# A hybrid RWKV-7 and RG-LRU layer on one core: row halves in turn, a padded matrix, other operand offsets, chunks and first loads

## The chip, the cores and the metric

The kernel runs on one core of a Trainium2 chip. The metric is device time in microseconds of one execution, the median of several runs. Engines are named as the profile names them: PE is TensorE's matmul, PEld its load of the stationary operand, DVE is VectorE, ACT is ScalarE, POOL is GpSimd, SP is SyncE, which issues nearly all DMAs.

## What is computed

One decoder layer over 256 tokens of width 2048: half a SwiGLU step, a mixing step with two groups of heads that share one input and one output projection, another half SwiGLU step, and a norm.

```python
h = h + 0.5 * swiglu(rms_norm(h, ffn1_norm), w_gate, w_up, w_down)     # 2048 -> 5632 -> 2048
p = rms_norm(h, mix_norm) @ w_in                                       # 2048 -> 5408
r, xw, k, v, xa, xg = split(token_shift(p[..., :3360]), (1024, 64, 1024, 1024, 64, 160))
w = -softplus(-(w0 + tanh(xw) @ w2)) - 0.5       # decay, low rank 64
a = sigmoid(a0 + xa @ a2)                        # rate, low rank 64
g = sigmoid(xg) @ g2                             # gate, low rank 160
y_rwkv = delta_rule_scan(r, exp(-exp(w)), k, v, a) * g                 # 16 heads of 64
y_lru = gated_linear_recurrence(p[..., 3360:])
h = h + concat(y_rwkv, y_lru) @ w_out                                  # 2048 -> 2048
h = h + 0.5 * swiglu(rms_norm(h, ffn2_norm), w_gate2, w_up2, w_down2)
return rms_norm(h, final_norm)
```

## The kernel before

**Products in three parts.** Weights and activations are float32. For the large products each is split into a high part in the format fp32r and a low part that holds the rest, and a product is high x high + high x low + low x high: three matmuls that add up in one PSUM bank. `weights` (line 47) loads a strip of a weight matrix, k tile by k tile (128 rows), into a `wst` buffer; ScalarE copies it to `whi` (line 73), VectorE subtracts to get `wlo` (line 74). There are three buffers of each. `kstep` k tiles share one DMA, `kop` k tiles one split.

**The large products.** In `rows_times` (line 85) a 128x128 block of the activations is stationary and up to 512 columns of weights move: used by both FFNs and by w_out. Each matmul there loads another stationary block than the one before or loads it again. In `columns_times` (line 97) the weights are stationary and 256 tokens move: the projections by w_in.

**The FFN** (line 164). The 5632 hidden columns are taken in chunks: four of 1024, then two of 768, each cut into pieces of at most 512. A chunk's gate product runs over 16 k tiles and 2 token tiles, then its up product. The product's hidden tile is transposed on TensorE (line 183, four transposes per k pair) in the middle of the next chunk's gate product, after k tile 7; the last chunk's after k tile 11 of the down product. The down product runs over 44 k tiles in pieces of 1024 or 512 columns.

**The start.** x comes in four quarters of 512 columns, which are transposed in halves (line 126, 16 transposes each, with the split to `xahi` and `xalo` on ScalarE and VectorE behind them). The first chunk's weights follow with k tiles 0 and 1 alone, then in pairs.

**The mixing stage** (line 825) runs steps of two halves of the heads in the order of line 874, between the eleven projections. `decays` (line 457) makes decay and rate: w2 lies on rows 0 to 63 of `w2a2`, a2 on rows 64 to 127, and each float32 matmul over 64 rows and 256 tokens is issued as two passes. `small()` hands out PSUM banks 6 and 7 in turn, `small(True)` banks 3 to 5. The gram products (line 574) and the chain of the recurrence (line 683 and on) also work on 64 rows. `rwkv_out` (line 722) multiplies by the gate: two matmuls for each of 8 blocks, over 128 rows of `g2a` and 32 rows of `g2b`.

**What sets the order.** A scheduler orders each engine's instructions from the program order and priorities. `high_priority(offset)` lets what is inside go ahead by that many places; `issue_after(x)` keeps it behind x. Each engine then works through its queue in order.

**Where tiles lie.** In the built program's memory map the bytes per partition are these: on the left, from below, `const` with `junk` (2048 bytes) in it, then the weight buffers `wst` at 22400, `whi` at 46976, 51072 and 55168, `wlo` at 59264, 63360 and 67456, then `xahi` at 71552 and `xalo` at 87936. In the first FFN `hThi` lies at 128896 and `hTlo` from 173952 to 219008. On the right, downward from 229344: `h2` at 212960 (16384 bytes), then the second FFN's `xbhi` at 180192 and `xblo` at 196576. The second FFN's last left tile ends at 178048.

Of the kernel before, what the change touches and what calls it, by code (L numbers as in the profile page):

```python
# [3 lines left out]

# [7 lines left out]
F32 = mybir.dt.float32  # L12
# [8 lines left out]
class Core:  # L21


    def __init__(self, ctx, tc, S, D, WMAX):
# [11 lines left out]
        self.h = None  # L36
        self.ones = self.const.tile([P, P], F32, name="ones")
# [9 lines left out]
    def weights(self, pieces, ktiles, kstep=2, kop=1, head=False):  # L47
# [4 lines left out]
        steps = [1, 1] if head else []  # L52
        while sum(steps) < len(ktiles):
            steps.append(min(kstep, len(ktiles) - sum(steps)))
        for k0, n in zip(itertools.accumulate([0] + steps), steps):
            with self.tc.high_priority(offset=4000):
# [11 lines left out]
                for j in range(0, n, kop):  # L68
# [4 lines left out]
                    self.last_split = nc.scalar.copy(hi[:, : m * width], src)  # L73
                    nc.vector.tensor_tensor(  # L74
                        lo[:, : m * width], src, hi[:, : m * width].bitcast(F32), ALU.subtract
                    )
# [8 lines left out]
    def rows_times(self, banks, xhi, xlo, kidx, whi, wlo, width, first, last):  # L85

        nc = self.nc
        for t in range(self.NT):
# [5 lines left out]
            for n, c, w in cuts:  # L94
                nc.tensor.matmul(banks[t][n][:, :w], b, whi[:, c : c + w], start=False, stop=last)  # L95
# [30 lines left out]
    def transposed_half(self, hf, gT, xhi, xlo, banks):  # L126

        nc = self.nc
        per = self.NK // 2
        for j in range(0, per, 2):  # L130
            bk = self.bank(banks[(j // 2) % len(banks)])
            for jj in range(2):
                k = hf * per + j + jj
# [6 lines left out]
            for jj in range(2):  # L140
                k = hf * per + j + jj
                src = bk[:, jj * 256 : jj * 256 + self.S]
                nc.scalar.activation(xhi[:, k, :], src, AF.Copy, scale=gT[:, k : k + 1])
                nc.vector.scalar_tensor_tensor(  # L144
                    xlo[:, k, :], src, gT[:, k : k + 1], xhi[:, k, :].bitcast(F32), ALU.mult, ALU.subtract
                )

# [16 lines left out]
def ffn(core, xhi, xlo, rstd, wg, wu, wd, after_first, after_down, fpool, down, head=False):  # L164
# [4 lines left out]
    while c < DFF:  # L169
        left = DFF - c  # L170
        w = 1024 if left >= 2 * 1024 or left <= 1024 else left // 2
        w = min(w, left)
        chunks.append((c, w))
        c += w
# [22 lines left out]
    for c0, w in chunks:  # L197
# [3 lines left out]
        for i, (k, hi, lo) in enumerate(core.weights([(wg, c0, w)], ks, head=head and c0 == 0)):  # L201
            core.rows_times(gb, xhi, xlo, k, hi, lo, w, i == 0, i == NK - 1)
            if i == NK // 2 - 1:
                for f in pending:
                    f()
                pending = []
# [18 lines left out]
    for piece, (c0, w) in enumerate(down):  # L225
# [3 lines left out]
        for i, (k, hi, lo) in enumerate(core.weights([(wd, c0, w)], list(range(NF)), 2048 // w, 1024 // w)):  # L229
# [18 lines left out]
class Mix:  # L248
# [20 lines left out]
    def consts(self):  # L269
# [132 lines left out]
        self.g2b = mc.tile([32, 1024], F32, name="g2b")  # L402
        nc.sync.dma_start(out=self.g2a, in_=d["rwkv_g2"][0, 0:128, :])
        nc.sync.dma_start(out=self.g2b, in_=d["rwkv_g2"][0, 128:160, :])
# [638 lines left out]
```

## Time and profile before

| | |
|---|---|
| median of 3 runs | 1979.71 us (1976.21 to 1979.80) |
| the profiled execution | 1979.79 us, of which the span from the first to the last instruction is 1978.1 us |
| TensorE busy | 1952.5 us, 99% of the span |
| VectorE, ScalarE busy | 1078.4 us (55%), 880.1 us (44%) |
| granted TensorE clock, mean | 0.996 of full speed |

An engine that is busy all the time sets the time; what the others do counts where it waits for them. The records of a few matmuls are missing from the trace, so counts over a stretch are taken from the program and times from landmarks.

### The profile page before, as it was taken

Reading aid. Unit: us, or ns where it says so; the run is one execution under the profiler, and the core shown is the slowest. Engines: PE = TensorE matmul, PEld = TensorE weight load, DVE = VectorE, ACT = ScalarE, POOL = GpSimd, SP = SyncE. Lnnn points to the kernel's source line nnn. Section 1 sums busy time; section 2 is a strip of 40 time slices with the busy share of each in tenths; the row PEclk is TensorE's granted clock in tenths of the full one; section 3 lists DMA queues with packets and bytes.
Section 4 is the critical chain, followed back from the end, with each engine's and each line's share of the span. In section 5 each row is a group of like instructions: output and inputs, shape, how many; then the busy total and the mean of one; then the engine's idle time right before and its main releaser. Section 6 shows DMA issues by size and latency. Waiting matters only on the chain.

```text
span 1978.1 us, 26035 instructions
## 1 busy us (share of the span) xinstructions
PE 1952.5 (99%) x10789; PEld 1652.5 (84%) x10789; DVE 1078.4 (55%) x1313; ACT 880.1 (44%) x1062; POOL 8.9 (0%) x52
## 2 busy tenths in 40 slices
PE   8999999999999999999999999999999999999997
PEld 6888888888888889898899878888888888888886
DVE  4455444544545447886684875444545455544543
ACT  4544434444434335544354554434443444443443
POOL 0000000000000001000000000000000000000000
PEclk9999999999999999999999999999999999999999
DMA  6555555566656556544342365555555556665553
GB/s 234 192 189 194 182 196 181 167 189 180 209 187 211 191 187 219 164 139 126 97 147 88 127 224 183 189 192 174 188 187 175 181 175 178 207 214 193 193 192 128
DMA packets 128639, 354.51 MB, mean 179 GB/s; under 512 B 21023, under 2 KB 23272, under 8 KB 128392
## 3 DMA queue, kind: packets, MB, share of 16 engines
q1 hardware_dynamic: 128200, 351.79, 55.4%
q8 instruction: 84, 1.38, 0.3%
q10 hardware_dynamic: 320, 1.06, 0.1%
q14 instruction: 35, 0.29, 0.0%
HBM read 347.05 MB, written 5.77 MB: 178 GB/s over the span
## 4 chain that ended last, share of the span: by engine, by line
PE 97%; DVE 1%; ACT 1%; DMA 0%; issue 0%; SPq 0%; DVEq 0%; ACTq 0%
PE bank L92 26%; PE bank L95 26%; PE bank L93 26%; PE bank L104 4%; PE bank L106 4%; PE bank L105 4%; PE bank L183 1%; PE bank L574 1%; PE bank L502 1%; PE bank L467 0%; PE bank L663 0%; PE bank L135 0%; PE bank L691 0%; PE bank L670 0%; DMA wst<-in_ffn_w_gate_dram 0%
## 5 line engine op out<-in xcount | busy, mean ns | idle before, releaser
L74 DVE TENSOR_TENSOR wlo<-wst,whi 128x1024 fp32r<-128x1024 f32 (+1 forms) x680 | 795.5, 1170 | 834.1 <-ACT whi L73 832.9
L73 ACT CAST whi<-wst 128x1024 fp32r<-128x1024 f32 (+1 forms) x680 | 685.8, 1009 | 1004.5 <-PE bank L95 867.3
L92 PE MATMUL bank<-whi,xahi 128*128 128x512 f32 (+1 forms) x896 | 337.2, 377 | 3.8 <-DVE xalo L144 3.6
L93 PE MATMUL bank<-wlo,xahi 128*128 128x512 f32 (+1 forms) x896 | 330.1, 375 | 1.1 <-DVE wlo L74 1.1
L92 PE MATMUL bank<-whi,xbhi 128*128 128x512 f32 (+1 forms) x768 | 289.5, 377 | 0.0
L93 PE MATMUL bank<-wlo,xbhi 128*128 128x512 f32 (+1 forms) x768 | 283.7, 377 | 0.0
L92 PE MATMUL bank<-whi,hThi 128*128 128x512 f32 x704 | 274.2, 390 | 0.0
L93 PE MATMUL bank<-wlo,hThi 128*128 128x512 f32 x704 | 274.0, 389 | 0.0
L95 PE MATMUL bank<-whi,xalo 128*128 128x512 f32 (+1 forms) x896 | 264.8, 376 | 0.0
L95 PE MATMUL bank<-whi,hTlo 128*128 128x512 f32 x704 | 231.4, 389 | 0.0
L95 PE MATMUL bank<-whi,xblo 128*128 128x512 f32 (+1 forms) x768 | 227.6, 377 | 0.0
L92 PEld LDWEIGHTS bank<-whi,xahi 128*128 128x128 f32 x896 | 168.7, 188 | 41.2 <-DVE xalo L144 4.0
L104 PE MATMUL bank<-xahi,whi 128*128 128x256 f32 x688 | 198.6, 289 | 1.0 <-DVE raw L437 1.0
L106 PE MATMUL bank<-xahi,wlo 128*128 128x256 f32 x688 | 197.4, 288 | 0.0
L105 PE MATMUL bank<-xalo,whi 128*128 128x256 f32 x688 | 196.8, 286 | 0.0
L93 PEld LDWEIGHTS bank<-wlo,xahi 128*128 128x128 f32 x896 | 168.6, 188 | 31.9 <-DVE wlo L74 1.5
L95 PEld LDWEIGHTS bank<-whi,xalo 128*128 128x128 f32 x896 | 159.8, 189 | 24.9
L92 PEld LDWEIGHTS bank<-whi,xbhi 128*128 128x128 f32 x768 | 144.5, 188 | 34.3
L93 PEld LDWEIGHTS bank<-wlo,xbhi 128*128 128x128 f32 x768 | 144.4, 188 | 28.7
L95 PEld LDWEIGHTS bank<-whi,xblo 128*128 128x128 f32 x768 | 135.8, 189 | 23.4
L92 PEld LDWEIGHTS bank<-whi,hThi 128*128 128x128 f32 x704 | 132.2, 188 | 27.4
L93 PEld LDWEIGHTS bank<-wlo,hThi 128*128 128x128 f32 x704 | 132.2, 188 | 27.3
(242 smaller groups left out, 1355.3 us busy)
## 6 DMA issues: line engine op xcount, KB each, us to landing
wst<-in_ffn_w_down_dram SPq DMA_DIRECT2D x88, 1024.0 KB, 5.0
wst<-in_ffn_w_up_dram SPq DMA_DIRECT2D x64, 1024.0 KB, 5.0
wst<-in_ffn_w_gate_dram SPq DMA_DIRECT2D x63, 1024.0 KB, 5.0
wst<-in_w_in_dram SPq DMA_DIRECT2D x40, 1024.0 KB, 5.2
wst<-in_ffn_w_gate_dram SPq DMA_DIRECT2D x32, 768.0 KB, 4.4
wst<-in_ffn_w_up_dram SPq DMA_DIRECT2D x32, 768.0 KB, 4.4
wst<-in_w_out_dram SPq DMA_DIRECT2D x16, 1024.0 KB, 5.5
wst<-in_w_in_dram SPq DMA_DIRECT2D x4, 640.0 KB, 4.3
```

What stands on the lines that cost most here:

```text
L73: self.last_split = nc.scalar.copy(hi[:, : m * width], src)
L74: nc.vector.tensor_tensor(lo[:, : m * width], src, hi[:, : m * width].bitcast(F32), ALU.subtract)
L92: nc.tensor.matmul(banks[t][n][:, :w], a, whi[:, c : c + w], start=first, stop=False)
L93: nc.tensor.matmul(banks[t][n][:, :w], a, wlo[:, c : c + w], start=False, stop=False)
L95: nc.tensor.matmul(banks[t][n][:, :w], b, whi[:, c : c + w], start=False, stop=last)
L104: nc.tensor.matmul(out, a, xhi[:, k, :], start=first, stop=False, skip_group_check=True)
L105: nc.tensor.matmul(out, a, xlo[:, k, :], start=False, stop=False, skip_group_check=True)
L106: nc.tensor.matmul(out, b, xhi[:, k, :], start=False, stop=last, skip_group_check=True)
L183: nc.tensor.transpose(bk[:, jj * 256 + t * P : jj * 256 + (t + 1) * P], hid[:, t, (j + jj) * P : (j + jj + 1) * P], core.ident,)
L502: self.nc.tensor.matmul(bk[0:8, :256], ind[:, j0 + j, :], src[:, j * 256 : (j + 1) * 256], start=j == 0, stop=j == 3)
L574: nc.tensor.matmul(bks[par][:, j * P : (j + 1) * P], BK[j // 2][rows, j % 2, c, :], KR[j // 2][rows, j % 2, c, :], start=True, stop=True,)
```

## The change

- `decays` takes the four blocks in pairs and issues a decay product (rows 0 to 63, a bank of `small(True)`) and a rate product (rows 64 to 127, a bank of `small()`) in turn.
- `g2b` becomes a tile of 128 rows, zero from row 32 on, and its matmul takes all 128 rows of the third block of the low-rank inputs.
- `junk` grows by 128 bytes and `h2` by 2016 bytes per partition, with no other use of them.
- The FFN's chunks are one of 512 columns and then five of 1024.
- `kop` and `kstep` follow from the width: 1 and 2 k tiles for 1024 columns, 2 and 4 for 512 and for 384. For the down product and the projections they come out as before.
- At the start the first weights, x's quarters and the next weights are issued in turn; x is transposed in quarters, the first ahead, each later one behind k tile 0, 1 or 2 of the first chunk; the splits of the first chunk's weights up to k tile 7 are kept behind the splits of x that `marks` holds.

```diff
@@ class Core
+        self.marks = []
...
-    def weights(self, pieces, ktiles, kstep=2, kop=1, head=False):
+    def weights(self, pieces, ktiles, head=False):
...
-        steps = [1, 1] if head else []
+        kop = self.WMAX // width
+        kstep = 2 * kop
+        steps = [1, 1, 2] if head else []
...
-            with self.tc.high_priority(offset=4000):
+            with self.tc.high_priority(offset={0: 9500, 1: 8700, 2: 8500}.get(k0, 4000) if head else 4000):
...
-                    self.last_split = nc.scalar.copy(hi[:, : m * width], src)
-                    nc.vector.tensor_tensor(
-                        lo[:, : m * width], src, hi[:, : m * width].bitcast(F32), ALU.subtract
-                    )
+                    with ExitStack() as behind:
+                        if head and 0 < k0 < 8:
+                            for mark in self.marks[4 * k0 - 1 if k0 < 3 else -1]:
+                                behind.enter_context(self.tc.issue_after(mark.ins))
+                        self.last_split = nc.scalar.copy(hi[:, : m * width], src)
+                        nc.vector.tensor_tensor(
+                            lo[:, : m * width], src, hi[:, : m * width].bitcast(F32), ALU.subtract
+                        )
...
-    def transposed_half(self, hf, gT, xhi, xlo, banks):
+    def transposed(self, k0, n, gT, xhi, xlo, banks):
...
+                self.marks.append((a, b))
...
@@ ffn
-        left = DFF - c
-        w = 1024 if left >= 2 * 1024 or left <= 1024 else left // 2
-        w = min(w, left)
+        w = (DFF - c) % 1024 or 1024
...
             core.rows_times(gb, xhi, xlo, k, hi, lo, w, i == 0, i == NK - 1)
+            if head and c0 == 0 and i in head:
+                with core.tc.high_priority(offset=3000), core.tc.issue_after(core.last_mm.ins):
+                    head[i]()
...
-        for i, (k, hi, lo) in enumerate(core.weights([(wd, c0, w)], list(range(NF)), 2048 // w, 1024 // w)):
+        for i, (k, hi, lo) in enumerate(core.weights([(wd, c0, w)], list(range(NF)))):
@@ Mix.consts
-        self.g2b = mc.tile([32, 1024], F32, name="g2b")
+        self.g2b = mc.tile([P, 1024], F32, name="g2b")
+        g.memset(self.g2b, 0.0)
...
-        nc.sync.dma_start(out=self.g2b, in_=d["rwkv_g2"][0, 128:160, :])
+        nc.sync.dma_start(out=self.g2b[0:32], in_=d["rwkv_g2"][0, 128:160, :])
@@ Mix.decays
-        for half, dst, bias in ((0, ld, self.w0h), (1, ta, self.a0h)):
-            rows = slice(64 * half, 64 * half + 64)
-            for j in range(0, 4, 2):
-                bk = self.small()
-                for a in range(2):
-                    jj = hf * 4 + j + a
+        for j in range(0, 4, 2):
+            bks = (self.small(True), self.small())
+            for a in range(2):
+                jj = hf * 4 + j + a
+                for half in range(2):
+                    rows = slice(64 * half, 64 * half + 64)
                     nc.tensor.matmul(
-                        bk[:, a * 256 : a * 256 + 256], self.w2a2[rows, jj * P : (jj + 1) * P],
+                        bks[half][:, a * 256 : a * 256 + 256], self.w2a2[rows, jj * P : (jj + 1) * P],
                         L[rows, 0, :], start=True, stop=True,
                     )
+            for a in range(2):
+                jj = hf * 4 + j + a
+                for bk, dst, bias in zip(bks, (ld, ta), (self.w0h, self.a0h)):
                     nc.scalar.activation(
...
@@ Mix.rwkv_out
-            nc.tensor.matmul(gb[:, :256], self.g2b[:, jj * P : (jj + 1) * P], L[0:32, 2, :], start=False, stop=True)
+            nc.tensor.matmul(gb[:, :256], self.g2b[:, jj * P : (jj + 1) * P], L[:, 2, :], start=False, stop=True)
@@ tile_hybrid_layer_kernel
-    junk = const.tile([P, HD], mybir.dt.bfloat16, name="junk")
+    junk = const.tile([P, HD + 64], mybir.dt.bfloat16, name="junk")
...
-                with tc.high_priority(offset=8000 if q < 2 else 0):
+                with tc.high_priority(offset=(9000, 8600, 8400, 8300)[q]):
...
-            with tc.high_priority(offset=8500):
-                norm_half(0, 0, *xa)
-            norm_half(0, 1, *xa)
+
+            def norm_quarter(q):
+                core.transposed(4 * q, 4, gT[:, :NK], *xa, ((2, 3), (4, 5), (6, 7))[q % 3])
+
+            with tc.high_priority(offset=8800):
+                norm_quarter(0)
...
-                first_norm, park, fpool, [(0, HD), (HD, HD)], head=True)
+                first_norm, park, fpool, [(0, HD), (HD, HD)], head={q: partial(norm_quarter, q + 1) for q in range(3)})
...
-        core.h = h2.tile([P, core.NT, D], F32, name="h2")
+        core.h = h2.tile([P, core.NT * D + 504], F32, name="h2")[:, : core.NT * D].rearrange("p (t d) -> p t d", t=core.NT)
```

## Rows read from the trace of the kernel before

**Rows 1.** The page: busy time by engine; the chain that ended last.

```profile
PE 1952.5 (99%) x10789; PEld 1652.5 (84%) x10789; DVE 1078.4 (55%) x1313; ACT 880.1 (44%) x1062; POOL 8.9 (0%) x52
...
PE 97%; DVE 1%; ACT 1%; DMA 0%; issue 0%; SPq 0%; DVEq 0%; ACTq 0%
```

**Rows 2.** Busy time in the mixing stage: stretch, its length, busy us by engine.

```profile
752.00:1177.00 425.00, 419.40 (x3621) 377.52 (x3620) 316.28 (x565) 213.61 (x312) 7.93 (x44) 0.99 0.47 147
```

**Rows 3.** Timeline of PE, start and length in us: first transposes of hidden tiles.

```profile
126.43 0.38 PE L183 MATMUL bank<-ident,hid 128*128 128x128 f32 x2
...
215.24 0.38 PE L183 MATMUL bank<-ident,hid 128*128 128x128 f32 x2
...
387.97 0.49 PE L183 MATMUL bank<-ident,hid 128*128 128x128 f32 x3
...
457.11 0.38 PE L183 MATMUL bank<-ident,hid 128*128 128x128 f32 x2
...
1335.99 0.38 PE L183 MATMUL bank<-ident,hid 128*128 128x128 f32 x2
...
1427.70 0.38 PE L183 MATMUL bank<-ident,hid 128*128 128x128 f32 x2
...
1605.38 0.38 PE L183 MATMUL bank<-ident,hid 128*128 128x128 f32 x2
...
1674.13 0.38 PE L183 MATMUL bank<-ident,hid 128*128 128x128 f32 x2
```

**Rows 4.** The chain in the first FFN's down product, at both ends of 384 matmuls.

```profile
541.84 1.31 PE bank L183 x12
...
630.67 0.16 PE bank L135
```

**Rows 5.** The chain at the first group of decay passes.

```profile
790.19 1.06 PE bank L467 x4
791.25 0.32 PE bank L104
791.56 0.12 PE bank L105
```

**Rows 6.** The chain at one block of the gate products.

```profile
998.73 0.43 PE bank L745 x2
999.16 0.62 PE bank L746 x2
999.78 0.32 PE bank L106
```

**Rows 7.** The chain at two groups of gram passes.

```profile
842.68 1.16 PE bank L574 x8
...
950.27 0.65 PE bank L574 x8
```

**Rows 8.** Timeline of POOL and of SP's queue: a memset, the load of g2b.

```profile
755.31 0.63 POOL L408 MEMSET lru_wa<- 64x512 f32 x1
...
790.74 0.49 SPq L404 DMA_DIRECT2D g2b<-in_rwkv_g_dram  x1
```

**Rows 9.** Timeline of the start, with the idle time before and its releaser.

```profile
5.10 4.01 PE L135 MATMUL bank<-ident,h 128*128 128x128 f32 x16 [1.09 <-DMA h<-in_x_dram]
...
7.14 1.57 PEld L135 LDWEIGHTS bank<-ident,h 128*128 128x128 f32 x8 [0.47 <-DMA h<-in_x_dram]
...
8.42 1.04 ACT L73 CAST whi<-wst 128x1024 fp32r<-128x1024 f32 x1 [5.86 <-DMA wst<-in_ffn_w_gate_dram]
...
9.50 1.23 DVE L74 TENSOR_TENSOR wlo<-wst,whi 128x1024 fp32r<-128x1024 f32 x1 [5.28 <-ACT whi L73]
...
10.64 0.48 DVE L144 SCALAR_TENSOR_TENSOR xalo<-bank,gT,xahi 128x256 fp32r<-128x256 f32 x1
...
12.70 0.79 PE L92 MATMUL bank<-whi,xahi 128*128 128x512 f32 x1 [3.59 <-DVE xalo L144]
```

**Rows 10.** The chain at the start.

```profile
13.49 0.43 PE bank L93
```

More of the change, by code (lines that the diff above doesn't have):

```diff
@@ L3 @@
 from contextlib import ExitStack
+from functools import partial
 import concourse.bass as bass
@@ L94, in rows_times @@
             for n, c, w in cuts:
-                nc.tensor.matmul(banks[t][n][:, :w], b, whi[:, c : c + w], start=False, stop=last)
+                self.last_mm = nc.tensor.matmul(banks[t][n][:, :w], b, whi[:, c : c + w], start=False, stop=last)
     def columns_times(self, bks, ntile, i, last, xhi, xlo, k, hi, lo):
@@ L124, in spread_rstd @@
         nc.vector.tensor_copy(self.rb, bk[:, :256])
-    def transposed_half(self, hf, gT, xhi, xlo, banks):
+    def transposed(self, k0, n, gT, xhi, xlo, banks):
         nc = self.nc
-        per = self.NK // 2
-        for j in range(0, per, 2):
+        for j in range(0, n, 2):
             bk = self.bank(banks[(j // 2) % len(banks)])
             for jj in range(2):
-                k = hf * per + j + jj
+                k = k0 + j + jj
                 for t in range(self.NT):
@@ L140, in transposed_half @@
             for jj in range(2):
-                k = hf * per + j + jj
+                k = k0 + j + jj
                 src = bk[:, jj * 256 : jj * 256 + self.S]
-                nc.scalar.activation(xhi[:, k, :], src, AF.Copy, scale=gT[:, k : k + 1])
-                nc.vector.scalar_tensor_tensor(
+                a = nc.scalar.activation(xhi[:, k, :], src, AF.Copy, scale=gT[:, k : k + 1])
+                b = nc.vector.scalar_tensor_tensor(
                     xlo[:, k, :], src, gT[:, k : k + 1], xhi[:, k, :].bitcast(F32), ALU.mult, ALU.subtract
                 )
+                self.marks.append((a, b))
     def sumsq(self, c0, w, acc, junk):
@@ L161, in rstd_of, with ffn @@
         nc.vector.reciprocal(rstd, tmp)
-def ffn(core, xhi, xlo, rstd, wg, wu, wd, after_first, after_down, fpool, down, head=False):
+def ffn(core, xhi, xlo, rstd, wg, wu, wd, after_first, after_down, fpool, down, head=None):
     nc, NT, NK, D, S = core.nc, core.NT, core.NK, core.D, core.S
@@ L200, in ffn @@
         gb = [[core.bank(t * nb + n) for n in range(nb)] for t in range(NT)]
-        for i, (k, hi, lo) in enumerate(core.weights([(wg, c0, w)], ks, head=head and c0 == 0)):
+        for i, (k, hi, lo) in enumerate(core.weights([(wg, c0, w)], ks, head=bool(head) and c0 == 0)):
             core.rows_times(gb, xhi, xlo, k, hi, lo, w, i == 0, i == NK - 1)
+            if head and c0 == 0 and i in head:
+                with core.tc.high_priority(offset=3000), core.tc.issue_after(core.last_mm.ins):
+                    head[i]()
             if i == NK // 2 - 1:
@@ L425, in project @@
             self.nproj += 1
-        for i, (k, hi, lo) in enumerate(core.weights(pieces, list(range(NK)), 4, 2)):
+        for i, (k, hi, lo) in enumerate(core.weights(pieces, list(range(NK)))):
             core.columns_times(bks, ntile, i, i == NK - 1, xhi, xlo, k, hi, lo)
@@ L933, in norm_half @@
     def norm_half(i, hf, xhi, xlo):
-        core.transposed_half(hf, gT[:, i * NK : (i + 1) * NK], xhi, xlo, (0, 1, 2, 3) if hf == 0 else (4, 5, 6, 7))
+        core.transposed(hf * NK // 2, NK // 2, gT[:, i * NK : (i + 1) * NK], xhi, xlo, (0, 1, 2, 3) if hf == 0 else (4, 5, 6, 7))
     def norm_rows(i, bank):
```

## The prediction

> **What bounds the kernel now.** I read the page's shares first: TensorE is busy 99% of the span, VectorE and ScalarE are not near it, and the chain that ended last is TensorE for 97% of its length [rows 1]. So the question for each edit is how many nanoseconds of TensorE's queue it removes; a faster transfer or eviction is worth nothing unless TensorE waits for it. The mixing stage looks busier with other things, so I asked for it alone: TensorE is busy 419.4 of 425.0 us there [rows 2], which leaves 5.6 us of waiting in all. A busy TensorE still need not run at its pace, so the next view is the pace: how long one weight-switching matmul takes in each stage.
>
> The pace comes from landmarks. Each chunk's hidden tile is transposed in the middle of the next chunk's gate product, so two neighbouring landmarks of 1024-wide chunks are 384 matmuls of 512 columns apart (half a gate, an up, half a gate: 96 + 192 + 96), and 16 transposes. Twelve of these take 1.31 us [rows 4], so sixteen 1.75. In the first FFN: 215.24 - 126.43 - 1.75 = 87.06 us, or 226.7 ns a matmul. In the second: 1427.70 - 1335.99 - 1.75 = 89.96 us, 234.3 ns [rows 3]. The reader should see that the same instructions with the same shapes take 7.6 ns more. The 768-wide chunks, cut into 512 + 256 columns, are 192 such pairs apart: (457.11 - 387.97 - 1.75) / 192 = 351.0 ns a pair in the first FFN, (1674.13 - 1605.38 - 1.75) / 192 = 349.0 in the second [rows 3]. One and a half 512-wide matmuls at 226.7 would be 340.0.
>
> **Why the second FFN is slower.** What differs is where the stationary operand lies. By the byte offsets told with the kernel, xa lies at 71552, a multiple of 128, xb at 180192, which is 96 beyond one. It is not the region: hThi and hTlo of the first FFN reach across it (128896 to 219008), and the down product that reads them needs (630.67 - 541.84 - 1.31) / 384 = 227.9 ns for k tiles 12 to 43, with 12 transposes at 109 ns taken off [rows 4]; the surplus over 226.7 is the two slow pieces at either end. So I take the odd offset as the cause.
>
> **The operands' offsets.** The 504 floats more in h2 put xb at 178176, and the 128 bytes more in junk move the weights and xa to 47104 and 71680: all multiples of 2048, and at the same distance from each other modulo 2048 as the first FFN's are now. So xb should take xa's pace. In the four 1024-wide chunks that is 4 x (89.96 - 87.06) = 11.6 us. For the pace at a multiple of 2048 itself the trace has no row (all fast operands lie 1920 beyond one); I take 226.7, the row of the same relative place.
>
> A rule of the Trainium skill speaks against this term: "SBUF — State Buffer", Specifications (TRN2), gives 16-byte cachelines as what an access pays for, and every offset here is a multiple of 32. By it moving xb changes nothing. The 7.6 ns of the rows above speak for some dependence that this rule doesn't have; it is the first rival.
>
> **The chunks.** 512 + 5 x 1024 in place of 4 x 1024 + 2 x 768: no 256-wide pieces. Per 768 chunk 192 x (351.0 - 340.0) = 2.1 us in the first FFN, 192 x (349.0 - 340.0) = 1.7 in the second; two each: 4.2 + 3.4 = 7.6 us. ScalarE and VectorE split the same columns (a 512-wide chunk is split two k tiles at a time), so the reserve of three split tiles is worth the same TensorE time. The projections, w_out and the down product get the steps that they had.
>
> **The decay and rate products.** 32 passes (16 fp32 matmuls of two passes), now in eight groups of four, all rows of a group in one half of the array. A group costs 1.06 us and its successor 0.32 instead of 0.12, so 1.26 [rows 5]; four passes at 0.216, half of what two passes over 128 rows take [rows 6], are 0.86, the rest is going into the 64-row form and out again. The change makes groups of eight, upper and lower in turn, each half with a bank of its own: four groups. Do halves run side by side? The gram products show both: eight passes in 1.16 us where one half's follow each other, 0.65 where the halves take turns [rows 7]. At that ratio, 0.56, eight decay passes cost 0.56 x (1.06 + 0.86) = 1.08, what four do now, and 4 x 1.26 = 5.0 us go. Bounds: 1.6 if nothing runs side by side (four switches of about 0.4 saved), 5.9 if the groups merge in pairs. I take 5.0, as the order in the program is that of the 0.65 row. The chain banks 3 to 5 are idle then, and ScalarE issues as many evictions.
>
> **Gate's second matrix.** Now two passes of 128 rows (0.43), two of 32 rows (0.62), and 0.32 for the successor [rows 6], which takes 0.12 elsewhere [rows 5]; with 128 rows 2 x 0.43 and 0.12. That is (0.62 - 0.43) + 0.20 = 0.39 us, eight times: 3.1. Lower bound 1.5, if the four of the second half only shorten TensorE's waiting. The padding adds a POOL memset of 128x1024; a 64x512 one takes 0.63 us [rows 8], so an estimate of 1.3 us, at about 755 us. SP's transfer of g2b waits for it, with the weight loads queued behind; but that transfer is issued at 790.74 [rows 8], 34 us later. Cost nothing; if the cover were gone, 1.3 us.
>
> **The first loads.** Now: x lands, 16 transposes run at 5.10, the first weights land at 8.42, and the first product starts at 12.70 because ScalarE and VectorE split weights between the evictions [rows 9]. The landmark gives the total: 126.43 less 2.5 x 43.5 us of products is 17.6 us lost at the front. After: 256 KB of weights precede x's first quarter. The second quarter, 512 KB more, is waited for until 7.14 [rows 9], 2.0 us behind the first, so 256 KB are 1.0 at most, and x lands between 5.1 and 6.1; I take 5.8. Four transposes (half of the 1.57 there), an eviction on each engine (0.48 on VectorE, and about the same ahead of it on ScalarE, rows 9) and the first product starts near 7.9. Six matmuls at the early 0.43 [rows 10], then quarters' transposes between k tiles: k 1 at 12, k 2 at 15 to 16 (its split now queues behind quarter 1's evictions: 1.04 + 1.23, rows 9), k 4 near 21.6 behind those of quarter 3. Four k tiles of 1.36 us are done by then, so 16.2 us are lost: 1.4 gained. Bounds: 5.9 gained if no split is late (7.9 + 24 transposes at 0.109 (rows 4) + 6 x 0.2 for the slow matmuls = 11.7), 1.5 lost if the 1 MB of k 4 to 7 lands late. I take 1.4, because in the order of the change each of these steps waits for the one before it.
>
> **The sum.** 11.6 + 7.6 + 5.0 + 3.1 + 1.4 = 28.7 us. The profiled execution took 1979.8 us for a span of 1978.1, and the median is 1979.7, so no shift between them: 1979.8 - 28.7 = 1951.1.
>
> **The rivals.**
> *The offset is not the cause* (the 16-byte rule of the page above would have it so): xb stays at 234.3. Then the second FFN's gate and up take 2112 x 0.2343 = 494.8 instead of 478.8, 16.0 less gained: 1967.1. For it: only one operand with an odd offset is in the trace. Against it: nothing else differs between the two FFNs. 6%.
> *Multiples of 2048 are slow* (the other side): weights and activations now start at the same round offsets, and if that collides, 6720 matmuls (2112 in each FFN's gate and up, 1056 in each down, 384 in w_out) pay xb's 7.6 ns: 51.1 us, so 2002.2. It decides from 28.7 us / 6720 = 4.3 ns, a pace of 231.0, on. For it: no row has such an offset. Against it: only a common shift of 128 bytes is made. 5%.
> *Multiples of 2048 are faster still*: 256 columns take about 0.12 us in the projections [rows 5], 512 take 226.7 ns, so some 13.3 ns of each don't depend on the width. If all went, 6720 + 2064 projection matmuls x 13.3 = 116.8 us: 1834. Both widths have the same part, so it looks like the weight switch. 4%.
> *The mixing stage gives nothing*: a new order of queues turns 8.1 us of saved TensorE work into waits: 1959.2. For it: VectorE is busy 316 of 425 us there; against it, TensorE waits only 5.6 [rows 2]. 5%.
>
> **How the numbers follow.** The forecast has 80%. Its bounds: gains of 11.6 + 7.6 + 5.9 + 3.1 + 5.9 = 34.1 give 1945.7, and 11.6 + 7.6 + 1.6 + 1.5 - 1.5 = 20.8 give 1959.0. Runs of the kernel before lie up to 3.5 us below their median, so I go from 1943 to 1963, which takes in the last rival and leaves the first three out. Faster by over 0.2% (4 us, about what a measurement of this kernel tells from no change): the forecast, rivals one, three and four, less a little for errors that add up: 0.93. Within: 0.02. Slower: 0.05.
>
> **What would show it.** Landmarks of all chunks in both FFNs 88.8 us apart where the chunk is 1024 wide; no 256-wide FFN matmul; groups of eight decay passes of about 1.06 us; gate's passes at 0.43 a pair with no slow successor; the first chunk's landmark at 16.2 + 2 x 21.8 + 21.8 = 81.5. A second-FFN pace near 234, or a first-FFN pace off 226.7, would prove the address term wrong.

## The result and the profile after

The changed kernel takes 1957.0 us (median of 4 runs, 1956.3 to 1959.1) against 1979.7 for the kernel before on the same chip: a ratio of 0.989, 95% interval 0.987 to 0.991. The forecast was 1951.1 with a range of 1943 to 1963. The direction and the range held; the gain is 22.7 us where 28.7 was forecast. The profiled execution has a span of 1957.2 us, 20.9 less than before.

TensorE is as full as before: busy 1928.7 us, 99% of the span (compare [rows 1]).

The landmarks, as in [rows 3], from the timeline of PE (start and length in us): the first transposes of a hidden tile, the first of all and two in the second FFN.

```profile
83.24 1.03 PE L189 MATMUL bank<-ident,hid 128*128 128x128 f32 x8
...
1371.22 1.91 PE L189 MATMUL bank<-ident,hid 128*128 128x128 f32 x16
1460.03 1.91 PE L189 MATMUL bank<-ident,hid 128*128 128x128 f32 x16
```

The second FFN's chunks now lie 1460.03 - 1371.22 = 88.81 us apart, where before they lay 91.71 apart: (88.81 - 1.75) / 384 = 226.7 ns a matmul, the pace of the first FFN. The first landmark should have been at 81.5 and is at 83.24.

The busy times of stretches (length, then busy us by engine; the third figure from the end is the granted clock as a share of full speed), first the mixing stage as in [rows 2]:

```profile
747.00:1172.00 425.00, 415.77 (x3629) 379.81 (x3628) 317.80 (x567) 213.35 (x313) 9.00 (x46) 0.99 0.47 148
```

```profile
22.00:26.00 4.00, 3.89 (x10) 3.11 (x11) 2.41 (x4) 0.69 (x1) 0.00 (x0) 0.57 0.37 96
...
880.00:889.00 9.00, 5.42 (x45) 5.22 (x45) 8.62 (x20) 2.51 (x3) 0.00 (x0) 1.00 0.59 167
889.00:893.00 4.00, 4.00 (x23) 4.00 (x23) 3.26 (x7) 2.31 (x6) 0.20 (x2) 0.57 0.96 294
```

In the mixing stage TensorE is now idle for 9.2 us where it was idle for 5.6. In the stretch before 889 VectorE is the busy one (8.62 of 9 us) and TensorE waits; behind that wait, and behind one at 20 to 22 us, the granted clock is 0.57 over 4 us, that is, most of the stretch was at 1.2 GHz.

Two more views: the timeline at the two groups of decay products, as in [rows 5], and the chain at a block of the gate, as in [rows 6].

```profile
784.92 3.41 PE L478 MATMUL bank<-lora_in,w2a 64*128 64x256 f32 x16
...
859.10 2.00 PE L478 MATMUL bank<-lora_in,w2a 64*128 64x256 f32 x16
```

```profile
998.04 0.43 PE bank L759 x2
998.47 0.43 PE bank L760 x2
998.90 0.12 PE bank L112
```

The gate came out as forecast: 0.43 twice, and a successor at 0.12. The decay products of the first half of the heads take 3.4 us, those of the second 2.0, though both are the same 16 passes.

**Where the time went, by stretches of the span.** The front and the first FFN, up to the first transposes behind its down product: 3.9 us shorter (forecast 5.6). The mixing stage, from its first transposes at 747.69 (751.63 before) to those behind the first half of w_out: 423.4 us after, 425.1 before, 1.7 shorter (forecast 8.1). From there to the last chunk's landmark: 15.4 shorter (forecast 15.0: 11.6 for xb, 3.4 for the chunks). Behind it: 0.2 longer. So the missing part is 6.4 us in the mixing stage and 1.7 at the front.

### The profile page after: what moved, and what is told of

Same layout as the page of the kernel before. It is cut to its first block, busy times and chain, and to the rows that moved or that the text cites. A ratio compares the mean times of both kernels' runs of the same rounds, so it can differ in the third digit from the quotient of the medians.

```text
span 1957.2 us, 25119 instructions
## 1 busy us (share of the span) xinstructions
PE 1928.7 (99%) x10405; PEld 1633.9 (83%) x10405; DVE 1073.1 (55%) x1278; ACT 873.7 (45%) x1027; POOL 9.8 (1%) x53
## 4 chain that ended last, share of the span: by engine, by line
PE 94%; DVE 3%; ACT 1%; issue 1%; DMA 1%; SPq 0%; DVEq 0%; ACTq 0%
PE bank L101 26%; PE bank L103 26%; PE bank L100 26%; PE bank L112 3%; PE bank L114 3%; PE bank L113 3%; DVE wlo L82 1%; PE bank L189 1%; PE bank L142 1%; PE bank L588 1%; PE bank L516 1%; PE bank L677 0%; DVE invw L630 0%; DVE inv L634 0%; PE bank L705 0%
## 5 line engine op out<-in xcount | busy, mean ns | idle before, releaser
L101 PE MATMUL bank<-wlo,xahi 128*128 128x512 f32 x832 | 325.2, 391 | 2.0 <-DVE wlo L82 2.0
L100 PE MATMUL bank<-whi,xahi 128*128 128x512 f32 x832 | 325.5, 392 | 1.4 <-ACT whi L81 1.2
L100 PE MATMUL bank<-whi,xbhi 128*128 128x512 f32 x704 | 274.3, 390 | 0.0
L101 PE MATMUL bank<-wlo,xbhi 128*128 128x512 f32 x704 | 274.1, 389 | 0.0
L103 PE MATMUL bank<-whi,xalo 128*128 128x512 f32 x832 | 264.0, 391 | 0.0
L103 PE MATMUL bank<-whi,hTlo 128*128 128x512 f32 x704 | 231.4, 389 | 0.0
L103 PE MATMUL bank<-whi,xblo 128*128 128x512 f32 x704 | 222.1, 389 | 0.0
L112 PE MATMUL bank<-xahi,whi 128*128 128x256 f32 x688 | 199.4, 290 | 3.8 <-DVE raw L447 3.8
L113 PE MATMUL bank<-xalo,whi 128*128 128x256 f32 x688 | 197.5, 287 | 0.0
L101 PEld LDWEIGHTS bank<-wlo,xahi 128*128 128x128 f32 x832 | 156.9, 189 | 35.1 <-DVE wlo L82 2.9
L100 PEld LDWEIGHTS bank<-whi,xahi 128*128 128x128 f32 x832 | 156.8, 189 | 34.5 <-ACT whi L81 1.6
L103 PEld LDWEIGHTS bank<-whi,xalo 128*128 128x128 f32 x832 | 156.8, 189 | 32.6
L103 PEld LDWEIGHTS bank<-whi,hTlo 128*128 128x128 f32 x704 | 132.1, 188 | 27.4
L101 PEld LDWEIGHTS bank<-wlo,xbhi 128*128 128x128 f32 x704 | 132.2, 188 | 27.2
L103 PEld LDWEIGHTS bank<-whi,xblo 128*128 128x128 f32 x704 | 132.2, 188 | 27.2
```

Of the source, the lines that this page charges most:

```text
L100: nc.tensor.matmul(banks[t][n][:, :w], a, whi[:, c : c + w], start=first, stop=False)
L101: nc.tensor.matmul(banks[t][n][:, :w], a, wlo[:, c : c + w], start=False, stop=False)
L103: self.last_mm = nc.tensor.matmul(banks[t][n][:, :w], b, whi[:, c : c + w], start=False, stop=last)
L112: nc.tensor.matmul(out, a, xhi[:, k, :], start=first, stop=False, skip_group_check=True)
L113: nc.tensor.matmul(out, a, xlo[:, k, :], start=False, stop=False, skip_group_check=True)
```

## Experiments on the operands' offsets

The forecast had taken the second FFN's pace from the odd offset of xb, and the change made the offsets of weights and activations multiples of 2048. Four kernels change only the two paddings.

`a1_no_h2_pad`:

```diff
-        core.h = h2.tile([P, core.NT * D + 504], F32, name="h2")[:, : core.NT * D]...
+        core.h = h2.tile([P, core.NT * D], F32, name="h2")[:, : core.NT * D]...
```

> The kernel after, without the 504 floats more in h2: xb goes back to byte 180192, 96 beyond a multiple of 128; everything else as in the kernel after. Theory (xb's offset sets the pace of the second FFN's gate and up): landmarks of the second FFN 384 x 0.2343 + 1.75 = 91.7 us apart, those of the first 88.8 as now; 2112 x 7.6 ns = 16.0 us more, so about 1973 us. Rival (the second FFN got faster by the new chunks or by the order of loads): 88.8 in both, about 1957.

`a2_h2_pad_8` and `a3_h2_pad_24` have `+ 8` and `+ 24` in place of `+ 504`.

> As the run before it, with 8 floats more in h2: xb at byte 180160, 64 beyond a multiple of 128. No row shows such an offset. If an operand has to start at a multiple of 128 bytes: 91.7 us between the second FFN's landmarks, about 1973. If a multiple of 64 is enough: 88.8, about 1957. If the cost grows with the distance, a value in between. I expect the first.

> 24 floats more in h2: xb at byte 180096, a multiple of 128 but 1920 beyond a multiple of 2048, while the weights stay at multiples of 2048. Theory (a multiple of 128 is what counts): 88.8 us between the second FFN's landmarks, about 1957. Rival (the multiple of 2048 of the change is what helped, or the same distance between weights and activations): 91.7, about 1973.

`a4_no_junk_pad`:

```diff
-    junk = const.tile([P, HD + 64], mybir.dt.bfloat16, name="junk")
+    junk = const.tile([P, HD], mybir.dt.bfloat16, name="junk")
```

> The other half of the padding undone: without the 128 bytes more in junk, so that the weights, xa and the other left operands lie 1920 beyond a multiple of 2048 as in the kernel before, while xb stays at a multiple of 2048. Theory (junk's padding does nothing for the pace): landmarks 88.8 us apart in both FFNs, about 1957. Rival (the relative place modulo 2048 counts): about 91.7 in the second FFN or in both, 1973 to 1990.

Measured, in one execution each: 1973.0, 1963.5, 1968.7 and 1970.0 us. Landmarks of the second FFN, from the timelines of a1, a2, a3 and a4 in this order:

```profile
1466.97 1.91 PE L189 MATMUL bank<-ident,hid 128*128 128x128 f32 x16
1558.31 1.91 PE L189 MATMUL bank<-ident,hid 128*128 128x128 f32 x16
```

```profile
1462.14 1.91 PE L189 MATMUL bank<-ident,hid 128*128 128x128 f32 x16
1551.78 1.91 PE L189 MATMUL bank<-ident,hid 128*128 128x128 f32 x16
```

```profile
1463.57 1.91 PE L189 MATMUL bank<-ident,hid 128*128 128x128 f32 x16
1554.55 1.91 PE L189 MATMUL bank<-ident,hid 128*128 128x128 f32 x16
```

```profile
1464.75 1.91 PE L189 MATMUL bank<-ident,hid 128*128 128x128 f32 x16
1555.73 1.91 PE L189 MATMUL bank<-ident,hid 128*128 128x128 f32 x16
```

That is 91.34, 89.64, 90.98 and 90.98 us apart, or 233.3, 228.9, 232.4 and 232.4 ns a matmul; the first FFN stays at 88.8 in all four. a1 shows that xb's place is worth some 14 us: 2112 matmuls of the second FFN at 6.6 ns more each, and 1973.0 against 1959.1 us in the two profiled executions. But a3 has xb on a multiple of 128 and is slow, and a4 has xb on a multiple of 2048 and is as slow. So the offset itself isn't the cause, and the theory that I went in with fell. What goes with all six values is the distance of xb, the stationary operand, from the weights that move: 0 in the kernel after, 96 bytes modulo 256 before (234.3), and 224, 192, 128 and 128 in a1 to a4. In the first FFN that distance is 0 in every kernel.

`p1_pace` measures it by itself, and the row patterns of the decay products as well. Its first part, in short:

```python
for k in range(6):                      # 72 matmuls for each pair (move, stat) of byte offsets
    for t in range(2):                  # a and b step by 512 bytes, as blocks of x do
        for st, w in ((a, whi0), (a, wlo0), (a, whi1), (a, wlo1), (b, whi0), (b, whi1)):
            nc.tensor.matmul(bank, st, w)
```

> Leaves out the whole layer: it only copies x to the output and times two things by themselves. First, 41 stretches of 72 matmuls (or 12 passes of six: stationary a, a, a, a, b, b as in the FFN) in which the stationary slices start a given number of bytes beyond the moving ones, modulo 2048. Second, 13 patterns of fp32 products over 64, 128 or 32 rows between full products, three times each. New theory, since the runs a2 to a4 went against a multiple of 128 (64 beyond: 89.64 us between landmarks, a multiple of 128 alone: 90.98, both offsets round but not the same: 90.97): what counts is the distance between the stationary and the moving operand. Then distance 0 gives 226.7 ns a matmul, 96 gives 234.3, 128 and 384 give 232.4, 448 gives 228.9, 480 gives 233.3, with a period of at most 512, since slices step by 512 bytes; a shift of both by the same amount changes nothing (226.7). Rival: the stationary operand's own place counts, then a shift of both by 1920 bytes gives 232.4 and a shift of the moving one alone 226.7. For the decay patterns: LULULULU in about 1.7 us with both switches, LLLLUUUU in about 3.3 (the first half as the gram products of two halves in turns, the second as 16 passes in a row); if halves don't run side by side for fp32 products, the same for both.

The timeline of PE in p1_pace. A stretch lasts from its start to the start of the next; in order the distances are 0, 4, 96, 128, 160, 192, 224, 256 and 288 bytes, then the moving and the stationary operand both shifted by 1920, then by 1920 and 2016:

```profile
20.91 16.52 PE L68 MATMUL six<-Z 128*128 128x512 f32 x72
37.27 16.89 PE L73 MATMUL six<-Z 128*128 128x512 f32 x72
...
121.01 17.02 PE L98 MATMUL six<-Z 128*128 128x512 f32 x72
137.87 16.89 PE L103 MATMUL six<-Z 128*128 128x512 f32 x72
154.60 16.96 PE L108 MATMUL six<-Z 128*128 128x512 f32 x72
171.40 16.66 PE L113 MATMUL six<-Z 128*128 128x512 f32 x72
187.89 16.96 PE L118 MATMUL six<-Z 128*128 128x512 f32 x72
204.69 16.49 PE L123 MATMUL six<-Z 128*128 128x512 f32 x72
221.02 16.95 PE L128 MATMUL six<-Z 128*128 128x512 f32 x72
...
453.65 16.49 PE L198 MATMUL six<-Z 128*128 128x512 f32 x72
469.97 17.02 PE L203 MATMUL six<-Z 128*128 128x512 f32 x72
486.83 16.50 PE L208 MATMUL one<-Z 128*128 128x512 f32 x72
```

Divided by 72: 227.2 ns at 0 (L68), 234.2 at 96 (L98), 232.4 at 128 (L103), 229.0 at 192 (L113), 233.3 at 224 (L118), 226.8 at 256 (L123). These are the paces of the layer before and of a1 to a4, within 0.5 ns. A common shift by 1920 bytes leaves 226.7 (L198), and 96 beyond that gives 234.2 (L203). The distances from 288 to 480 bytes, in steps of 32, repeat the paces of those from 32 to 224 within 0.2 ns. So in this order of six matmuls the distance between the two operands modulo 256 bytes sets the pace, and where they lie does not.

> Leaves out the whole layer (it copies x to the output). A finer sweep of the first part of p1_pace: for each distance of the stationary operand from the moving one from 0 to 252 bytes in steps of 4, 48 matmuls of 512 columns and 48 of 256. From p1_pace: 512 columns take 226.7 ns at 0 and at 240, 228.8 at 192, 230.7 to 234.3 at nine other places; 256 columns take 120.0 at 0 and 128, 117.3 to 118.7 at 64, 96 and 384 (128 more than a multiple of 256, but 118.7 where 128 gave 120.0, so for 256 columns the period is not settled). Open: is 226.7 the least for 512 columns, and how near to 0 must the operands be. If the pace follows the distance smoothly, the places from 240 to 252 are at 226.7 and those from 4 to 28 near 231 to 233. If single places hit the streams' turns, values under 226.7 turn up; a place that gave 220 would be worth 6720 x 6.7 ns = 45 us in the layer.

The sweep found nothing under 226.7 ns for 512 columns; that value came at 0, 120 and 132 bytes, and most other distances gave 230 to 236. One value of p1_pace didn't come again: 226.7 at 496 bytes, but 228.7 at 240, the same distance modulo 256. For 256 columns 0 is not the best. The rows of p2_sweep at 0 and at 64 bytes, and what follows each:

```profile
32.50 5.91 PE L73 MATMUL short<-Z 128*128 128x256 f32 x48
38.25 11.31 PE L78 MATMUL six<-Z 128*128 128x512 f32 x48
...
301.72 5.61 PE L233 MATMUL short<-Z 128*128 128x256 f32 x48
307.18 11.37 PE L238 MATMUL six<-Z 128*128 128x512 f32 x48
```

(38.25 - 32.50) / 48 = 119.8 ns at 0, and 113.8 at 64. Here 64 bytes gave 117.8 in p1_pace and 113.3 in p2_sweep (over the steady part), so away from 0 the distance alone doesn't fix the pace. What else does stays open.

## Experiments on the decay products and the mixing stage

The second part of p1_pace gives the price of row patterns (L: a product over rows 0 to 63, U: over rows 64 to 127, two passes each), always with 12 full products of 0.12 us between them. From the start of one repeat to the start of the next, for LL, LULU and LULULULU:

```profile
654.95 1.13 PE L275 MATMUL LL<-low 64*128 64x256 f32 x4
657.64 1.13 PE L282 MATMUL LL<-low 64*128 64x256 f32 x4
...
663.01 1.14 PE L296 MATMUL LULU<-low 64*128 64x256 f32 x8
665.70 1.13 PE L303 MATMUL LULU<-low 64*128 64x256 f32 x8
...
679.19 2.00 PE L338 MATMUL LULULULU<-low 64*128 64x256 f32 x16
682.74 2.00 PE L345 MATMUL LULULULU<-low 64*128 64x256 f32 x16
```

Less the 1.44 of the full products: 1.25 us for the old group of four passes, 1.25 for eight in turns, 2.11 for sixteen in turns. The same reading of LLLLUUUU, with the halves one behind the other, gives 3.07 (1.7 and 3.3 had been expected for the last two). So halves in turns do run side by side, and the forecast's price of a new group, 1.08 and 0.20 for its successor, was right. In the kernel after, the second half's 16 passes take the 2.00 of LULULULU, 2.1 net. The first half's take 3.41, 3.5 net: there the scheduler had put the four products of one row half ahead of the four of the other, and only one or two of the sixteen passes run beside another. The old order has four groups of 1.25 in each half, so the change saved 5.0 - 3.5 = 1.5 us in the first and 5.0 - 2.1 = 2.9 in the second, 4.4 in place of 5.0. That isn't where 6.4 us went.

`d1_old_decays` undoes that part of the change alone (the loops of the diff's `Mix.decays` in their old order).

> The decay and rate products in the old order again (all four groups of one half, then of the other), everything else as in the kernel after. By the sum of the prediction 5.0 us slower than the kernel after (1962.0); by what the two decay stages of the trace after took (1.5 us saved in the first, 2.9 in the second) 4.4 us slower (1961.4). Theory: TensorE's time saved there was taken back by waits for VectorE's evictions 20 us behind it, so only 0 to 2 us slower than the kernel after, 1957 to 1959, and the wait of 3.85 us for the eviction of a projection at 885 us is shorter by about what the products take more.

Measured: ratio 0.988 (0.986 to 0.990), the mixing stage 422.6 us (745.73 to 1168.37) where the kernel after has 423.4. The old order is no slower, so the 4.4 us were worth nothing at the end. (The intervals of the ratios are some 3 us wide to either side. Where kernels differ by less, the lengths of the stage in the traces say more.) The waits of TensorE in the mixing stage (us in total, times, longest), first of the kernel before, then after, then d1:

```profile
PE bank L104 <- DVE raw L437: 1.0, 1, 1.0
```

```profile
PE bank L112 <- DVE raw L447: 3.8, 2, 3.6
...
PE bank L516 <- ACT bk L531: 0.6, 1, 0.6
```

```profile
PE bank L112 <- DVE raw L447: 1.0, 1, 1.0
```

L112 (L104 before) is the first matmul of a projection; its bank is freed by L447, an eviction that VectorE gets to behind the inversion of the gram blocks and the weights' low parts, which keep it busy nearly without a gap (35.9 of the 37 us from 851 to 888). That inversion starts when the gram blocks, whose products TensorE ends at 841.86, have gone out to DRAM and come back. The chain of the kernel after, from there to the product that waits:

```profile
842.95 2.86 DMA scr<-gram
...
845.96 3.58 DMA inv<-scr
...
887.95 0.61 DVE raw L447
...
888.61 0.39 PE bank L112
```

Measured from the mixing stage's first transposes, this product starts at 751.63 + 141.4 before, 747.69 + 140.9 after, 745.73 + 141.7 in d1 and 744.62 + 141.8 in b3_turns below. TensorE's work ahead of it differs by several us between these kernels, the product's start by 0.9. The inversion starts 101.4 to 102.7 us into the stage in these four, and the product 39 to 40 us behind it: VectorE sets it. The second half's decay products, 111 us into the stage, lie beside that chain and can't shorten it. The first half's lie ahead of the gram products, but of their 1.5 us only 0.5 arrive there: the last group of these starts 93.0 us into the stage in the kernel after and 93.5 in d1. The direct proof, a kernel with less work for VectorE there, was not run.

`m1_four_banks` takes the wait's condition away, one more bank for the projections and one fewer for the chain:

```diff
-        return self.core.bank(3 + self.nbank[1] % 3 if chain else 6 + self.nbank[0] % 2)
+        return self.core.bank(4 + self.nbank[1] % 2 if chain else 6 + self.nbank[0] % 2)
...
-            bks.append(core.bank(self.nproj % 3))
+            bks.append(core.bank(self.nproj % 4))
```

> The projections of the mixing stage take turns on four PSUM banks in place of three, and the chain's small products on two in place of three. Theory (what TensorE saved in the mixing stage is waited for at the projections' evictions): the waits of L112 for the eviction of L447 (3.85 us at 885, 0.46 at 797) shrink, the half-clock stretch behind the first goes with it (1.5 us), and the kernel is 2 to 5 us faster than the kernel after, 1952 to 1955. Rival (VectorE itself is the bound there, or the chain needs its third bank): the wait moves to the next product that VectorE feeds, and the time stays at 1957, or rises by up to 3 us.

1959.8 us, ratio 0.991 (0.989 to 0.992), the mixing stage 424.1 us: the rival held. The wait moved to the next product that VectorE and ScalarE feed, which starts 146.4 us into the stage here and 147.0 in the kernel after; the chain to it runs over VectorE's raw and k and ScalarE's bk, not over a bank:

```profile
PE bank L516 <- ACT bk L531: 3.8, 2, 2.8
```

`f1_marks` concerns the front:

```diff
-                            for mark in self.marks[4 * k0 - 1 if k0 < 3 else -1]:
+                            for mark in self.marks[4 * k0 - 1 if k0 < 3 else 11]:
```

> The splits of the first FFN's k tiles 4 to 7 are placed behind the evictions of x's third quarter only, no longer behind the fourth's; everything else as in the kernel after. Theory (the order of these splits, not the transfer, is what TensorE waits for at 20 to 22 us, 0.97 + 0.36 us): both waits go, the evictions of the fourth quarter come later instead, and the first landmark lies at 80 to 82 instead of 83.2: 1.5 to 3 us faster than the kernel after, 1954 to 1955.5. Rival: the transposes of the last quarter wait for their evictions instead, and nothing is gained.

The waits at the front of the kernel after, from the timeline (in brackets the idle time before, and what ended it), as in [rows 9]:

```profile
20.85 0.74 PE L100 MATMUL bank<-whi,xahi 128*128 128x512 f32 x2 [0.97 <-ACT whi L81]
22.11 0.50 PE L101 MATMUL bank<-wlo,xahi 128*128 128x512 f32 x1 [0.36 <-DVE wlo L82]
```

In f1_marks both are gone and the first landmark lies at 78.83. Ratio 0.988 (0.987 to 0.990), 1955.2 us: 1.9 us under the kernel after, within the 1.5 to 3 of the theory, though the intervals overlap. Of the 4.4 us at the landmark a part belongs to the clock: in this execution the slow pace of the start, 0.43 us a matmul, ended earlier than in the kernel after. Against d1, where it ended as early, the landmark is 2.5 us ahead. The low clock from 22.5 to 26.0 us isn't in every execution: a3, a4 and d1 have the waits without it, and their first landmarks are at 80.6, 81.3 and 81.3, the place that was forecast.

`b2_shift64` and `b2_shift192` put the findings together: f1's mark, the old decays, and

```diff
-                    hi = self.wpool.tile([P, self.WMAX], F32R, name=self.name("whi"), tag="whi")
+                    hi = self.wpool.tile([P, self.WMAX + 64], F32R, name=self.name("whi"), tag="whi")[:, shift:]
...
-        for i, (k, hi, lo) in enumerate(core.weights(pieces, list(range(NK)))):
+        for i, (k, hi, lo) in enumerate(core.weights(pieces, list(range(NK)), shift=16)):
```

with the same for `wlo`, and `shift=48` in the second.

> Built from the kernel after, with the old order of the decay products and f1's mark, and one new edit: the weight tiles are 64 floats longer and the projections of the mixing stage put their weights 16 floats (64 bytes) into them, so that the stationary weights lie 64 bytes beyond the moving activations, modulo 256. For that space the two diagonal tiles of rms norm move to the first FFN's pool, and h2's padding is 56 floats, which keeps xb, as all operands of the FFNs, at a distance of 0 modulo 256, though no longer modulo 2048. Without the new edit, 1957.0 - 1.9 (f1) - 0.7 (d1, mixing stage alone) = 1954.4. Theory (the distance sets the pace of the 2064 projection matmuls of 256 columns too): they take 113.3 to 117.8 ns in place of 120.0, the two values of 64 bytes in the sweeps, 4.5 to 13.8 us less, so 1940.6 to 1949.9 if TensorE's waits in the mixing stage don't grow, and landmarks of both FFNs stay 88.8 apart. Rival 1 (VectorE bounds the stretch around 885 us and takes the gain back as it did with the decays): projections at 113 to 118 ns but 1951 to 1954.5. Rival 2 (a distance of 0 modulo 2048 is needed): FFN landmarks 90 to 92 apart, 1970 or more.

> The same with a distance of 192 bytes in the projections (48 floats). The fine sweep gave 113.3 ns for 256 columns at 192, as at 64; the coarse one didn't try it. Theory: 113.3 to 118, 1940 to 1950. Which of the two distances is better is open; where the pace at other distances than 0 hangs on where in their turns the streams start, the two kernels differ by that and not by a rule.

1950.9 and 1951.1 us, ratios 0.986 (0.984 to 0.988 and 0.987): the fastest versions here. The landmarks of both FFNs stay 88.8 apart although the weight buffers now start 4352 bytes from each other, a multiple of 256 and not of 2048, so 256 is enough. A projection without a break in b2_shift64, first and last of 46 matmuls:

```profile
806.88 0.28 PE L112 MATMUL bank<-xahi,whi 128*128 128x256 f32 x1
...
811.99 0.28 PE L112 MATMUL bank<-xahi,whi 128*128 128x256 f32 x1
```

(811.99 - 806.88) / 45 = 113.6 ns. Over all projections the mean is 115.7 in the first kernel and 117.2 in the second, against 119.8: 2064 matmuls, 8.5 and 5.4 us less TensorE work. The mixing stage takes 420.2 and 418.2 us, 2.4 and 4.5 less than d1. So of this gain, too, a part went into the wait (2.1 us for L112 in b2_shift64, against 1.0 in d1; its product starts 140.3 us into the stage in both) and into a stretch of low clock behind it, which b2_shift64 has (883.5 us) and b2_shift192 hasn't. From 914 to 921 us, too, b2_shift64 was granted 0.51 of the clock and b2_shift192 0.76, so what parts the two is the clock as much as the distance. Both kernels came out 1 us above the times expected of them: the distance did its part, but the first rival, VectorE, was nearer.

`b3_turns` puts the decay products of the change back into b2_shift64 and forces the turns (each product inside `issue_after` of the one before).

> b2_shift64 with the decay and rate products of the change back in, and this time in turns in both halves of the heads: each product is put behind the one before it, lower, upper, lower, upper. Nothing is left out. By p1_pace a group of eight passes in turns costs 1.25 us, so four of them 5.0 in place of the 10.0 of the old order's eight groups (1.25 each): the 5.0 us of the prediction, on TensorE. Theory (VectorE bounds the stretch that ends at 885 us, so TensorE waits there for what it saved before): the first half's 2.5 us become a longer wait of L112 or L516 at 885, the second half's lie in the same stretch, and the time stays within 2 us of b2_shift64 (1950.9): 1949 to 1953. Rival (the decay products were simply not in turns in the kernel after, and that alone lost the gain): 1945.9, and the waits at 885 as long as in b2_shift64 (2.1 us).

Both groups now run as LULULULU, 2.00 us each, and the waits grow:

```profile
787.97 2.00 PE L482 MATMUL bank<-lora_in,w2a 64*128 64x256 f32 x16
```

```profile
PE bank L112 <- DVE raw L447: 3.7, 1, 3.7
PE bank L520 <- ACT bk L535: 3.1, 1, 3.1
```

1952.7 us, ratio 0.987 (0.986 to 0.989): with the forecast's 5.0 us of TensorE work really gone, the kernel isn't faster than with the old order. Its mixing stage takes 421.6 us, 1.4 more than in b2_shift64: the 5.0 us went into 1.6 more at L112 and 3.1 at L520, and the 5 us behind the latter (803 to 808) were granted 0.66 of the clock. The rival's 1945.9 is out.

## Why the forecast was right, and where it was wrong

- **Address term, 11.6 us: the size was right, the cause was not.** I wrote that the odd offset is the cause, and took 226.7 because xb got "the same relative place" as the first FFN's operands. a3, a4 and p1_pace show that only the second half of that sentence counts. The change put both operands on round offsets, and so at distance 0; that the wrong cause gave the right number is luck. With padding to a multiple of 128 alone I would have forecast 11.6 us and got 2.9 of them (a3's 90.98 against 91.71, four times). The first rival was right that the offset isn't the cause, but its 234.3 ns and 1967.1 us are out. The rivals on multiples of 2048 fall with p1_pace: a common shift does nothing.
- **Chunks, 7.6 us:** no 256-wide piece is left, and the chunks are 88.8 apart. In the second FFN the two terms together gave 15.4 against 15.0, and the 3.9 at the front and in the first FFN fit 4.2 and a front that gave 0.3 back. No run undoes the chunks alone.
- **Front, 1.4 us:** forecast step by step (first product 7.9, measured 7.85; first landmark 81.5, measured 81.3 in a4 and d1). In the profiled execution the landmark came 1.7 us later, and d1's rows show the clock as what differs: the slow pace of the start lasted longer (the product behind the last wait of ScalarE's splits starts at 20.85 us, in d1 at 19.59), and the 4 us behind it were granted 0.57; a shorter second wait gave 0.9 back. The sum had neither. f1 shows that the wait itself came from the order of the splits.
- **Gate, 3.1 us of TensorE work:** as forecast in each block (0.43, 0.43, 0.12). The memset took 1.07 us and g2b's transfer was issued 35 us behind it, so the padding cost nothing, as forecast. Undoing it alone was not tried, but d1 has the gate's change with the old decays: its mixing stage is 2.5 us shorter than that of the kernel before, 2.8 counted from the product at 141 us on. Four of the eight blocks lie between that product and a product of the linear recurrence, from the timelines of PE in before and d1:

```profile
1022.12 0.48 PE L773 MATMUL bank<-xc,lru_wa 128*128 128x256 f32 x1 [0.50 <-DVE xc L769]
```

```profile
1014.94 0.48 PE L784 MATMUL bank<-xc,lru_wa 128*128 128x256 f32 x1 [0.50 <-DVE xc L780]
```

  Measured from that product, 129.1 us before and 127.5 in d1: 1.6 us, four times 0.39. So most of this term reached the end of the stage.
- **Decays, 5.0 us: the step that failed.** The price of a group was right (1.25 in p1_pace). Two things were not. The order in the program is not the order in TensorE's queue, which cost 0.6. And I set the whole sum against the end because TensorE waits only 5.6 us in the stage. That number says how little TensorE waits, not how little more it would take for VectorE to set the time: at the product that starts 141 us into the stage TensorE already waited for VectorE before the change, 1.0 us (L104's row), as in d1. Of its 4.4 us the kernel after brings 0.8 past that wait, against d1, and loses them again to a stretch of low clock. d1 and b3 show that nothing of this term reached the end.
- **The mixing stage as a whole:** the rival "gives nothing" was nearer (1.7 of 8.1), for its own reason. 7.5 us of work went, and the waits of L112 and L516 grew by 3.4. Against the kernel before, the kernel after is 0.5 us ahead at the product at 141 us (all that the decays gave), 2.1 ahead at the one of the recurrence (1016.12; the gate's first four blocks), and 0.5 ahead 45 us later: from 1043 to 1047 us it was granted 0.57 of the clock, where the kernel before had all of it, which cost 1.5. The rest of the gate gives 1.2 more, in all 1.7. a2 has that stretch of low clock too; a1, a3, a4, f1 and d1 have not.

## What to carry to other kernels

Before crediting saved work to the end of the kernel, ask in the same stretch for the second busiest engine: where it works without a gap up to a point that the first one waits for, nearly all that is saved beside it becomes waiting. Follow that engine's chain back to where it starts, since only work ahead of that can move it. Compare the pace of equal instructions in two stages, and when it differs, look at where the two operands lie to each other and not at one of them; two sizes of padding, each alone, tell these apart. An order that a scheduler makes has to be read from the trace or forced.

## What the runs showed of the hardware

- The distance between the stationary and the moving operand modulo 256 bytes sets the pace of back-to-back matmuls that each load a stationary block: 512 columns of fp32r at 226.7 ns at distance 0, up to 234.3 at 96 and single values to 243 in the fine sweep; 256 columns at 120.0 at distance 0 and down to 113.3 at 64 or 192. Away from 0 the same distance can give different paces (for 256 columns 117.8 and 113.3 at 64 bytes, for 512 columns 226.7 and 228.7 at 240).
- Products over different halves of the rows run wholly side by side when they alternate: eight passes cost 1.25 us, as four in one half do. Going into the 64-row form and out of it costs about 0.39 of that (1.25 less four passes of 0.216).
- A fall of the granted clock to 1.2 GHz isn't a fixed consequence of a wait: behind the front's waits it fell in the kernel after (TensorE was busy 2.78 of the 4 us from 18 to 22) and not in d1 (busy 1.74 of 4). What decides stays open. Where it fell under full work, 4 us granted at 0.57 cost some 1.5 us (matmuls of 0.21 us in place of 0.12 from 889 to 893).
